# Stick-breaking attention: one PSUM bank of transposes for 256 queries of two heads instead of 512 queries of one

## The chip, the cores and the metric

One core of one Trainium2 chip. The metric is device time in microseconds (us) of one execution of the whole program; of the kernel before there are three such times, and one further execution was run under the profiler.

## What is computed

One encoder layer over 2048 tokens of width 1024. Stage 1 projects the input and runs eight RWKV-7 heads, stage 2 is stick-breaking attention over eight heads of 64, stage 3 is the output projection and a squared-ReLU MLP. The change is in stage 2, whose reference is (float32 throughout):

```python
for blk in range(T // Q_BLOCK):
    z = jnp.einsum('bhqd,bhkd->bhqk', q[:, :, start:end], k[:, :, :end]) * scale
    causal = jnp.arange(end)[None, :] < (start + jnp.arange(Q_BLOCK))[:, None]
    log_beta = jax.nn.log_sigmoid(z)
    log_keep = jnp.where(causal, log_beta - z, 0.0)
    log_a = log_beta + lax.cumsum(log_keep, axis=3, reverse=True) - log_keep
    att = jnp.where(causal, jnp.exp(log_a), 0.0)
    outs.append(jnp.einsum('bhqk,bhkd->bhqd', att, v[:, :, :end]))
```

The last line is the value product: for every query a weighted sum of the values of all earlier keys.

## The kernel before

Stage 2 (`stage2`, from L244) works on two heads at a time (a head pair `hp`, four of them), on 512 queries at a time (`b`, four blocks), and for each of these on 512 keys at a time (`j` from `b` down to 0). That makes 4 x (1+2+3+4) = 40 blocks: 16 diagonal ones (`j==b`), where only keys up to the query count, and 24 full ones.

`front` (L265) takes 128 queries (`i`, four per block). TensorE (PE) multiplies them with up to 512 keys for both heads (L271, tile `z`, two PSUM banks; the two heads take rows 0 to 63 and rows 64 to 127 of the array). On a diagonal block a mask is added (L273). ScalarE (ACT) makes two sigmoids of it (L275 `keep`, L277 `ga`), VectorE (DVE) the running product along the keys (L281 `E`, one scan per head), GpSimd (POOL) the product `ga*E` in place (L282). `ga` then holds the attention weights, queries in the partitions. It has 9 buffers of both heads, `z` has 2, `E` 6.

`back` (L285) takes 128 of the block's keys (`kt`, four per block). For each head PE transposes the 128x128 pieces of `ga` of all four `i` into one PSUM bank (L294, tile `tr`, 128 keys x 512 queries, two banks in turn), and the bank is copied to SBUF (tile `th`, 4 buffers): every fourth copy by DVE (L297), the others by ACT (L298). When both heads are through, PE multiplies the values with `th` and adds into `OT` (L301; head 0 into partitions 0 to 63, head 1 into partitions 64 to 127 of one bank). On a diagonal block `kt` needs only the queries from `128*kt` on, so the widths are 512, 384, 256 and 128. `finish` (L302) moves `OT` out after the last block of a head pair.

`step` (L313) issues the `front` of a new block and the `back` of the block before it in turn, `i` by `i`. That is the order in which the program is written. A scheduler then puts the instructions of each engine into a fixed order by a planned timeline; each engine runs its own queue in that order, and waits on semaphores for the others. In the trace a float32 matmul is two records (two passes), with a weight load each; a transpose is one record.

Of the kernel before, what the change touches and what calls it, by code (L numbers as in the profile page):

```python
# [8 lines left out]
F32 = mybir.dt.float32  # L9
# [234 lines left out]
def stage2(tc,consts,kd,qd,vd,sbd,cfg=None):  # L244

    nc=tc.nc; V_=nc.vector; A=nc.scalar; P=nc.gpsimd; TE=nc.tensor
    g=dict(GA=9,E=6,TH=4,QB=3,DV=4)
    g.update(cfg or {})
    with ExitStack() as ctx:
        sp=ctx.enter_context(tc.tile_pool(name="s2",bufs=1,reuse_waits="tile"))  # L250
        pz=ctx.enter_context(tc.tile_pool(name="p2z",bufs=1,reuse_waits="tile",space=PS))
        pp=ctx.enter_context(tc.tile_pool(name="p2",bufs=1,reuse_waits="tile",space=PS))
        pt=ctx.enter_context(tc.tile_pool(name="p2t",bufs=1,reuse_waits="tile",space=PS,side="right"))

        keeps=[sp.tile([128,2,513],F32,name=f"keep{i}") for i in range(2)]
        for k in keeps: P.memset(k[:,:,512:513],1.0)

        pad=pp.tile([128,1],F32,name="pad"); V_.memset(pad,0.0)
        kv={}; cnt=[0,0]
        def load(hp,j):  # L260
            K=sp.tile([128,512],F32,name=f"K{hp}{j}"); V=sp.tile([128,4,128],F32,name=f"V{hp}{j}")
            nc.sync.dma_start(out=K,in_=kd[hp][:,512*j:512*j+512])
            nc.sync.dma_start(out=V,in_=vd[hp][:,4*j:4*j+4])
            kv[hp,j]=(K,V)
        def front(b,hp,j,Q,carry,i):  # L265

            n=f"{b}{hp}{j}"; K=kv[hp,j][0]
            W=128*(i+1) if j==b else 512; o=512-W
            z=pz.tile([128,2,512],F32,tag="z",name=f"z{n}{i}",bufs=2)
            for h in range(2):  # L270
                TE.matmul(z[:,h,0:W],lhsT=Q[64*h:64*h+64,128*i:128*i+128],rhs=K[64*h:64*h+64,0:W],start=True,stop=j<b,skip_group_check=True)  # L271
            if j==b:
                for h in range(2): TE.matmul(z[:,h,W-128:W],lhsT=consts['identr'],rhs=consts['cmask'],start=False,stop=True,skip_group_check=True)  # L273
            s=keeps[cnt[0]%2]; cnt[0]+=1
            A.activation(s[:,:,o:512],z[:,:,0:W],AF.Sigmoid,scale=-0.125)  # L275
            ga=sp.tile([128,2,512],F32,tag="ga",name=f"ga{n}{i}",bufs=g['GA'])
            A.activation(ga[:,:,o:512],z[:,:,0:W],AF.Sigmoid,scale=0.125)  # L277
            E=sp.tile([128,2,513],F32,tag="E",name=f"E{n}{i}",bufs=g['E'])
            for h in range(2):
                init=1.0 if j==b else carry[i][h]  # L280
                V_.tensor_tensor_scan(E[:,h,o:513][:,::-1],s[:,h,o:513][:,::-1],pad.to_broadcast([128,W+1]),init,ALU.mult,ALU.bypass)  # L281
            P.tensor_tensor(out=ga[:,:,o:512],in0=ga[:,:,o:512],in1=E[:,:,o+1:513],op=ALU.mult)  # L282
            carry[i]=[E[:,h,o:o+1] for h in range(2)]
            return ga,o
        def back(b,hp,j,gas,OT,kt):  # L285

            n=f"{b}{hp}{j}"; V=kv[hp,j][1]
            i0=kt if j==b else 0; q0=128*i0
            ths=[]
            for h in range(2):  # L290
                tr=pt.tile([128,512],F32,tag="tr",name=f"tr{n}{kt}{h}",bufs=2)
                for i in range(i0,4):
                    ga,o=gas[i]
                    TE.transpose(tr[:,128*i:128*i+128],ga[:,h,o+128*kt:o+128*kt+128],consts['ident'])  # L294
                th=sp.tile([128,512],F32,tag="th",name=f"th{n}{kt}{h}",bufs=g['TH'])
                cnt[1]+=1
                if cnt[1]%g['DV']==0: V_.tensor_copy(out=th[:,q0:],in_=tr[:,q0:])  # L297
                else: A.copy(th[:,q0:],tr[:,q0:])  # L298
                ths.append(th)
            for h in range(2):  # L300
                TE.matmul(OT[64*h:64*h+64,q0:],lhsT=V[:,kt,64*h:64*h+64],rhs=ths[h][:,q0:],start=j==b and kt==0,stop=j==0 and kt==3,skip_group_check=True)  # L301
        def finish(b,hp,OT):  # L302
            n=f"{b}{hp}"
            ots=sp.tile([128,512],F32,tag="ots",name="ots"+n,bufs=2)
            V_.tensor_copy(out=ots,in_=OT)
            o=pt.tile([128,4,128],F32,tag="tr",name="o"+n,bufs=2)
            for i in range(4): TE.transpose(o[:,i],ots[:,128*i:128*i+128],consts['ident'])
            osb=sp.tile([128,4,128],F32,tag="osb",name="osb"+n,bufs=2)
            A.copy(osb,o)  # L309
            nc.sync.dma_start(out=sbd[512*b:512*b+512,128*hp:128*hp+128].rearrange("(i p) d -> p i d",i=4),in_=osb)  # L310

        late=[None]
        def step(new):  # L313
            prev,late[0]=late[0],new
            for i in range(4):
                if new:
                    b,hp,j,Q,carry,gas,st=new
                    gas.append(front(b,hp,j,Q,carry,i))
                if prev:
                    b,hp,j,Q,carry,gas,st=prev  # L320
                    if j==b and i==0: st.append(pp.tile([128,512],F32,tag="OT",name=f"OT{b}{hp}",bufs=1))
                    back(b,hp,j,gas,st[0],i)
                    if j==0 and i==3: finish(b,hp,st[0])
        for b in range(4):
            for hp in range(4):
                load(hp,b)
                Q=sp.tile([128,512],F32,tag="Q",name=f"Q{b}{hp}",bufs=g['QB'])
                nc.sync.dma_start(out=Q,in_=qd[hp][:,512*b:512*b+512])
                carry=[None]*4; st=[]
                for j in range(b,-1,-1): step((b,hp,j,Q,carry,[],st))  # L330
        step(None)
# [334 lines left out]
def hybrid_block(tc, x, smalls, w_in, wd, wa, wg, g1, g2, gnw, gnb, w_out, w_up, w_down, gf, out):  # L666
    nc = tc.nc
    with ExitStack() as ctx:
        cp = ctx.enter_context(tc.tile_pool(name="c", bufs=1))
        dp = ctx.enter_context(tc.tile_pool(name="dr", bufs=1, space=bass.MemoryType.DRAM))  # L670
        c = mk_consts(tc, cp)
        dram = lambda name, shape: dp.tile(shape, F32, name=name)
        kd, qd = dram("kd", [4, 128, T]), dram("qd", [4, 128, T])
        vd = [dram(f"vd{h}", [128, 16, 128]) for h in range(4)]
        scr = {k: [[dram(f"scr{k}{b}{h}", [4, 4, 128, 32]) for h in range(2)] for b in range(4)] for k in "AX"}
        yd, vrd, gd, sbd = (dram(n, [T, 512]) for n in ("yd", "vrd", "gd", "sbd"))
        bond = dram("bond", [T, 8])
        x2d = dram("x2d", [T // 2, D])
        sb_consts(tc, cp, c)
        c["gain"] = cp.tile([128, 4], F32, name="gain")  # L680
        nc.sync.dma_start(out=c["gain"], in_=smalls[:, 34:38])
        with tc.tile_pool(name="c1", bufs=1, reuse_waits="tile") as c1:
            rw_consts(tc, c1, c, smalls, wd, wa)
            stage1(tc, c, x, w_in, kd, qd, vd, scr, yd, vrd, bond, gd, wg, g1)
        stage2(tc, c, kd, qd, vd, sbd)
        stage3(tc, c, x, (yd, vrd, bond, gd, sbd), w_out, g2, w_up, w_down, gf, gnw, gnb, c["gain"], out, x2d)
# [40 lines left out]
```

## Time and profile before

| | |
|---|---|
| three runs | 3447.58 us median, 3442.96 to 3448.63 |
| the profiled execution | 3452.84 us; its span, first to last instruction, 3450.8 us |
| stage 2 in that span | about 1120 to 1785 us |
| granted TensorE clock, mean of the span | 0.969 (1.0 is 2.4 GHz) |

A timeline line has the start in us, the time in us that the merged records take together, engine, line, operation, output<-input and the count of records; in brackets the idle time of the engine before it and what ended it. Records of successive matmuls overlap at their ends, so the price of a group on PE is read from its start to the start of the next group, not from its own length. "PEld" is the weight load. A groups line has the count, the busy time in us, the mean of one record in ns, and the idle time before it by what ended it.

### The profile page before, as it was taken

Reading aid. Unit: us, or ns where it says so; the run is one execution under the profiler, and the core shown is the slowest. Engines: PE = TensorE matmul, PEld = TensorE weight load, DVE = VectorE, ACT = ScalarE, POOL = GpSimd, SP = SyncE. Lnnn points to the kernel's source line nnn. Section 1 sums busy time; section 2 is a strip of 40 time slices with the busy share of each in tenths; the row PEclk is TensorE's granted clock in tenths of the full one; section 3 lists DMA queues with packets and bytes.
Section 4 is the critical chain, followed back from the end, with each engine's and each line's share of the span. In section 5 each row is a group of like instructions: output and inputs, shape, how many; then the busy total and the mean of one; then the engine's idle time right before and its main releaser. Section 6 shows DMA issues by size and latency. Waiting matters only on the chain. (4 is left out here: it accounts for less than half of the span.)

```text
span 3450.8 us, 44556 instructions
## 1 busy us (share of the span) xinstructions
PE 3288.2 (95%) x16992; PEld 2403.2 (70%) x16992; DVE 1999.8 (58%) x3111; ACT 1194.3 (35%) x2252; POOL 1245.6 (36%) x1089
## 2 busy tenths in 40 slices
PE   8999989999997899999968999999999999999998
PEld 6677768777776433333326878888888878888887
DVE  4773574575473555565647655555555655555556
ACT  4434444444441566666642221111111321111112
POOL 5444444444440434444436632222222332222223
PEclk9999999999996899999988999999999999999999
DMA  3342342342231400000025421111111231111111
GB/s 99 100 126 66 95 120 72 88 124 73 83 99 31 134 16 13 13 10 7 4 73 183 141 92 49 49 49 49 49 49 49 93 121 46 47 48 49 49 49 61
DMA packets 146726, 239.24 MB, mean 69 GB/s; under 512 B 50000, under 2 KB 58192, under 8 KB 146512
## 3 DMA queue, kind: packets, MB, share of 16 engines
q1 hardware_dynamic: 146512, 236.39, 21.8%
q8 instruction: 134, 2.20, 0.3%
q14 instruction: 80, 0.66, 0.1%
HBM read 190.14 MB, written 46.20 MB: 68 GB/s over the span
## 5 line engine op out<-in xcount | busy, mean ns | idle before, releaser
L160 DVE TENSOR_TENSOR acc<-acc,dn 128x512 f32<-128x512 f32 x512 | 344.7, 685 | 413.7 <-PE dn L32 407.3
L282 POOL TENSOR_TENSOR ga<-ga,E 128x1024 f32<-128x1024 f32 (+3 forms) x160 | 274.7, 1726 | 381.5 <-ACT ga L277 272.2
L301 PE MATMUL OT<-th,V 128*64 128x512 f32 (+3 forms) x640 | 299.5, 554 | 3.0 <-DVE th L297 3.0
L145 ACT ACTIVATE r<-up 128x512 f32<-128x512 f32 x128 | 75.6, 592 | 615.4 <-PE up L32 615.4
L281 DVE TENSOR_TENSOR_SCAN E<-keep,E,pad 128x513 f32<-128x513 f32 x192 | 232.1, 1264 | 62.6 <-ACT keep L275 62.6
L294 PEld LDWEIGHTS tr<-ident,ga 128*128 128x128 f32 x1088 | 115.5, 141 | 206.4 <-issue 197.9
L148 DVE TENSOR_TENSOR m<-r 128x512 f32<-128x512 f32 x128 | 190.9, 1492 | 113.6 <-ACT r L145 113.6
L294 PE MATMUL tr<-ident,ga 128*128 128x128 f32 x1088 | 189.3, 289 | 1.0 <-ACT osb L309 1.0
L271 PE MATMUL z<-K,Q 64*128 64x512 f32 (+3 forms) x640 | 161.3, 589 | 25.3 <-ACT ga L277 17.0
L275 ACT ACTIVATE keep<-z 128x1024 f32<-128x1024 f32 (+3 forms) x160 | 144.7, 905 | 97.4 <-PE z L273 32.6
L298 ACT COPY th<-tr 128x512 f32<-128x512 f32 (+2 forms) x240 | 127.1, 535 | 129.2 <-PE tr L294 128.6
L149 DVE TENSOR_TENSOR gl<-m,gh 128x512 fp32r<-128x512 f32 x128 | 148.4, 1160 | 11.6 <-ACT gh L146 0.9
L277 ACT ACTIVATE ga<-z 128x1024 f32<-128x1024 f32 (+3 forms) x160 | 141.0, 895 | 31.5 <-PE tr L294 27.3
L281 DVE TENSOR_TENSOR_SCAN E<-keep,pad 128x129 f32<-128x129 f32 (+3 forms) x128 | 97.4, 806 | 66.9 <-ACT keep L275 55.6
L297 DVE COPY th<-tr 128x512 f32<-128x512 f32 (+1 forms) x80 | 46.2, 577 | 137.6 <-PE tr L294 137.2
L301 PEld LDWEIGHTS OT<-th,V 128*64 128x64 f32 x640 | 61.1, 134 | 92.7 <-issue 41.9
L532 DVE TENSOR_TENSOR tm<-Am,Xs 128x240 f32<-128x240 f32 (+27 forms) x248 | 110.9, 447 | 23.4 <-DMA Am<-scrA 17.2
L383 POOL TENSOR_TENSOR wls<-wfs,whs 128x512 fp32r<-128x512 f32 x64 | 84.6, 1322 | 104.0 <-ACT whs L382 96.8
L533 DVE TENSOR_TENSOR Xs<-Xs,tm 128x240 f32<-128x240 f32 (+27 forms) x248 | 114.3, 461 | 6.3
L30 PE MATMUL ips<-hT,whs 128*128 128x512 f32 x256 | 106.8, 417 | 0.5 <-ACT whs L382 0.5
L32 PE MATMUL ips<-hT,wls 128*128 128x512 f32 x256 | 105.9, 414 | 0.9 <-POOL wls L383 0.9
L30 PE MATMUL op<-wo,yh 128*128 128x512 f32 x256 | 103.1, 403 | 3.0 <-ACT yh L116 3.0
(1265 smaller groups left out, 8677.4 us busy)
## 6 DMA issues: line engine op xcount, KB each, us to landing
wfs<-w_in SPq DMA_DIRECT2D x64, 256.0 KB, 2.9
x<-x SPq DMA_DIRECT2D x32, 256.0 KB, 3.0
wfr<-w_in SPq DMA_DIRECT2D x32, 256.0 KB, 2.8
wfk<-w_in SPq DMA_DIRECT2D x32, 256.0 KB, 2.7
wfv<-w_in SPq DMA_DIRECT2D x32, 256.0 KB, 2.8
wfsv<-w_in SPq DMA_DIRECT2D x32, 256.0 KB, 2.9
x<-x SPq DMA_DIRECT2D x16, 512.0 KB, 3.4
out<-fo SPq DMA_DIRECT2D x32, 256.0 KB, 2.5
```

What stands on the lines that cost most here:

```text
L30: nc.tensor.matmul(ps,lhsT=lh,rhs=rh,start=first,stop=False)
L148: V.tensor_tensor(out=m,in0=r,in1=r,op=ALU.mult)
L149: V.tensor_tensor(out=gl[:,bl],in0=m,in1=gh[:,bl].bitcast(F32),op=ALU.subtract)
L160: V.tensor_tensor(out=a,in0=a,in1=ps,op=ALU.add)
L271: TE.matmul(z[:,h,0:W],lhsT=Q[64*h:64*h+64,128*i:128*i+128],rhs=K[64*h:64*h+64,0:W],start=True,stop=j<b,skip_group_check=True)
L275: A.activation(s[:,:,o:512],z[:,:,0:W],AF.Sigmoid,scale=-0.125)
L277: A.activation(ga[:,:,o:512],z[:,:,0:W],AF.Sigmoid,scale=0.125)
L281: V_.tensor_tensor_scan(E[:,h,o:513][:,::-1],s[:,h,o:513][:,::-1],pad.to_broadcast([128,W+1]),init,ALU.mult,ALU.bypass)
L282: P.tensor_tensor(out=ga[:,:,o:512],in0=ga[:,:,o:512],in1=E[:,:,o+1:513],op=ALU.mult)
L294: TE.transpose(tr[:,128*i:128*i+128],ga[:,h,o+128*kt:o+128*kt+128],consts['ident'])
L298: else: A.copy(th[:,q0:],tr[:,q0:])
L301: TE.matmul(OT[64*h:64*h+64,q0:],lhsT=V[:,kt,64*h:64*h+64],rhs=ths[h][:,q0:],start=j==b and kt==0,stop=j==0 and kt==3,skip_group_check=True)
```

## The change

Instead of one bank per head with all queries, `back` now makes one bank per half of the queries (`u`, 256 queries) with both heads side by side. A half that lies wholly ahead of `kt` on a diagonal block is left out. The bank is copied in one step, and both heads' value products, now 256 queries wide, follow that copy. The copies go to DVE at three places in eight instead of two in eight.

```diff
-    g=dict(GA=9,E=6,TH=4,QB=3,DV=4)
+    g=dict(GA=9,E=6,TH=4,QB=3,DV=(1,4,7))
...
-            ths=[]
-            for h in range(2):
-                tr=pt.tile([128,512],F32,tag="tr",name=f"tr{n}{kt}{h}",bufs=2)
-                for i in range(i0,4):
-                    ga,o=gas[i]
-                    TE.transpose(tr[:,128*i:128*i+128],ga[:,h,o+128*kt:o+128*kt+128],consts['ident'])
-                th=sp.tile([128,512],F32,tag="th",name=f"th{n}{kt}{h}",bufs=g['TH'])
+            for u in range(2):
+
+                c0=max(i0,2*u)
+                if c0>=2*u+2: continue
+                tr=pt.tile([128,2,256],F32,tag="tr",name=f"tr{n}{kt}{u}",bufs=2)
+                for h in range(2):
+                    for i in range(c0,2*u+2):
+                        ga,o=gas[i]
+                        TE.transpose(tr[:,h,128*(i-2*u):128*(i-2*u)+128],ga[:,h,o+128*kt:o+128*kt+128],consts['ident'])
+                th=sp.tile([128,2,256],F32,tag="th",name=f"th{n}{kt}{u}",bufs=g['TH'])
+                q=slice(128*(c0-2*u),256); qq=slice(128*c0,256*u+256)
                 cnt[1]+=1
-                if cnt[1]%g['DV']==0: V_.tensor_copy(out=th[:,q0:],in_=tr[:,q0:])
-                else: A.copy(th[:,q0:],tr[:,q0:])
-                ths.append(th)
-            for h in range(2):
-                TE.matmul(OT[64*h:64*h+64,q0:],lhsT=V[:,kt,64*h:64*h+64],rhs=ths[h][:,q0:],start=j==b and kt==0,stop=j==0 and kt==3,skip_group_check=True)
+                if cnt[1]%8 in g['DV']: V_.tensor_copy(out=th[:,:,q],in_=tr[:,:,q])
+                else: A.copy(th[:,:,q],tr[:,:,q])
+                for h in range(2):
+                    TE.matmul(OT[64*h:64*h+64,qq],lhsT=V[:,kt,64*h:64*h+64],rhs=th[:,h,q],start=j==b and kt==0 and u==0,stop=j==0 and kt==3 and u==1,skip_group_check=True)
```

The prediction also speaks of two other groups of matmuls, in stage 1: L574 writes its eight heads in turn into partitions 0 to 63 and 64 to 127, L579 writes its eight heads all into the same 64 partitions.

```python
574:                    TE.matmul(Sp[64*j:64*j+64,h//2],lhsT=BT[cc][:,e,j],rhs=UV[cc][:,e,h],start=h<2,stop=True,skip_group_check=True)
579:                    TE.matmul(X[vb:vb+64,h],lhsT=P1[cc][:,e,h%2,cr:cr+64],rhs=UV[cc][:,e,h],start=False,stop=h==7,skip_group_check=True)
```

## Rows read from the trace of the kernel before

**Rows 1.** Busy time of each engine by stretch: stage 2.

```profile
core 0: us, PE busy (x) PEld busy (x) DVE busy (x) ACT busy (x) POOL busy (x), PEclk, DMA share, GB/s
1120.00:1785.00 665.00, 632.42 (x2570) 254.60 (x2568) 381.15 (x417) 398.79 (x578) 274.66 (x160) 0.98 0.08 26
```

**Rows 2.** Groups by line and shape, stage 2.

```profile
L301 PE MATMUL OT<-th,V 128*64 128x512 f32 x448 | 237.5, 618 | 0.0
L281 DVE TENSOR_TENSOR_SCAN E<-keep,E,pad 128x513 f32<-128x513 f32 x192 | 232.1, 1264 | 62.6 <-ACT keep L275 62.6
L298 ACT COPY th<-tr 128x512 f32<-128x512 f32 x176 | 104.0, 591 | 119.6 <-PE tr L294 119.4
L297 DVE COPY th<-tr 128x512 f32<-128x512 f32 x48 | 32.9, 685 | 113.1 <-PE tr L294 113.1
L301 PEld LDWEIGHTS OT<-th,V 128*64 128x64 f32 x640 | 61.1, 134 | 92.7 <-issue 41.9 <-ACT th L298 31.6 <-DVE th L297 13.8
```

**Rows 3.** Timeline of a full block's back, head pair 0 of b=2.

```profile
1316.20 1.07 PE L301 MATMUL OT<-th,V 128*64 128x512 f32 x2
1316.36 0.58 ACT L298 COPY th<-tr 128x512 f32<-128x512 f32 x1 [0.56 <-PE tr L294]
1317.20 0.66 PE L294 MATMUL tr<-ident,ga 128*128 128x128 f32 x4
1317.79 1.07 PE L301 MATMUL OT<-th,V 128*64 128x512 f32 x2
```

**Rows 4.** Timeline of PE on a diagonal block: the narrower groups.

```profile
1305.21 0.86 PE L301 MATMUL OT<-th,V 128*64 128x384 f32 x2
1306.00 0.44 PE L294 MATMUL tr<-ident,ga 128*128 128x128 f32 x2
...
1308.59 0.65 PE L301 MATMUL OT<-th,V 128*64 128x256 f32 x2
1309.16 0.33 PE L294 MATMUL tr<-ident,ga 128*128 128x128 f32 x1
1309.42 1.13 PE L271 MATMUL z<-K,Q 64*128 64x512 f32 x4
...
1311.32 0.43 PE L301 MATMUL OT<-th,V 128*64 128x128 f32 x2
1311.68 0.66 PE L294 MATMUL tr<-ident,ga 128*128 128x128 f32 x4
```

**Rows 5.** Timeline of PE in stage 1: L574 and L579.

```profile
252.30 0.69 PE L574 MATMUL Sp<-UV,BT 128*64 128x64 f32 x16
252.82 1.10 PE L579 MATMUL Xp<-UV,P 128*64 128x64 f32 x16
253.85 0.33 PE L612 MATMUL tri<-ident,x 128*128 128x128 f32 x1
```

**Rows 6.** Timeline, end of a head pair: both heads' products side by side.

```profile
1324.15 1.93 PE L301 MATMUL OT<-th,V 128*64 128x512 f32 x4
1324.25 0.69 DVE L297 COPY th<-tr 128x512 f32<-128x512 f32 x1 [5.31 <-PE tr L294]
1325.00 0.19 PEld L301 LDWEIGHTS OT<-th,V 128*64 128x64 f32 x2 [0.66 <-DVE th L297]
```

**Rows 7.** Timeline of PE: `z` of two heads over 256 keys, and what follows.

```profile
1341.69 0.70 PE L271 MATMUL z<-K,Q 64*128 64x256 f32 x4
1342.33 0.44 PE L273 MATMUL z<-cmask,identr 128*128 128x128 f32 x2
```

**Rows 8.** Timeline where a new query block begins (b=2).

```profile
1328.31 9.50 DVE L281 TENSOR_TENSOR_SCAN E<-keep,E,pad 128x513 f32<-128x513 f32 x8 [1.50 <-ACT keep L275]
1331.00 1.13 PE L271 MATMUL z<-K,Q 64*128 64x512 f32 x4 [0.70 <-ACT ga L277]
...
1335.22 1.13 PE L271 MATMUL z<-K,Q 64*128 64x512 f32 x4 [1.02 <-ACT ga L277]
```

**Rows 9.** Groups, whole span: the weight loads of L574.

```profile
L574 PEld LDWEIGHTS Sp<-UV,BT 128*64 128x64 f32 x512 | 20.9, 158 | 14.2 <-issue 7.1 <-ACT UV L570 6.0 <-ACT pmr L429 0.4
```

## The prediction

> **What bounds the kernel now.** I read the busy time by stretch first, because only stage 2 changes. Over its 665 us PE is busy 632 us, ACT 399, DVE 381, POOL 275, and the granted clock is 0.98 [rows 1]. So PE is the engine to watch. The groups by line then say what fills it: the value products of L301 [rows 2]. The timeline shows how PE goes through a full block: a product of one head, four transposes, a product, with no gap [rows 3]. The price of a group is the distance to the start of the next one: 1.00 us for a 512-wide product, 0.59 for four transposes [rows 3]; 0.79, 0.57 and 0.36 us for products 384, 256 and 128 wide, and 0.26 for one transpose [rows 4]. By differences a product costs about 0.15 us plus 0.0017 per column, a transpose group 0.15 plus 0.11 each, so two cost 0.37 and three 0.48.
>
> Today the two heads' products stand apart: each waits for its own copy, and transposes fill the time between. The change puts them next to each other. All turns on whether two products that use different halves of the array's columns run at the same time.
>
> **The change part by part.** *Do neighbours overlap?* No line of stage 2 shows it. Where both heads do stand together the four records take 1.93 us, nearly twice one product's 1.07, but the second head's weight load starts only when its DVE copy is through (1324.25 + 0.69 = 1324.94, load at 1325.00) [rows 6], so that proves nothing. Stage 1 has the same form, 128 rows by 64 columns, both ways: L574, alternating between the column halves, gets 16 records off in 0.52 us; L579, always in one half, needs 1.03 us [rows 5]. Two halves run side by side at half the price. So a pair of 256-wide products should cost hardly more than one alone, 0.57 us. The dearer bound is `z`, two heads side by side in the rows, 0.64 us at 256 columns [rows 7]; the dearest is one after the other, 0.57 + 256 x 0.0017 = 1.00 us. I take 0.57, as L574 has the very form and `z` has another.
>
> *Products.* Removed: 320, of which 224 are 512 wide (24 full blocks x 8, 16 diagonal ones x 2) and 32 of each narrower width: 224 x 1.00 + 32 x (0.79 + 0.57 + 0.36) = 279 us. Added: 288 pairs, 256 of them 256 wide (24 x 8 + 16 x 4) and 32 with 128: 256 x 0.57 + 32 x 0.36 = 157 us. Difference -122 us, all on PE. With the price of `z` (0.64, and 0.07 more for the narrow ones too) it is -101; with no overlap 256 x 1.00 + 32 x 0.57 = 274, or -5.
>
> *Transposes.* Their number stays 1088, in fewer groups: before 224 x 0.59 + 32 x (0.48 + 0.37 + 0.26) = 168, after 256 x 0.59 + 32 x 0.37 = 163 us: -5.
>
> *Weight loads.* 640 become 1152. One takes 134 ns [rows 2], a pass over 256 columns 213 (half of 0.0017 x 256), so a load is hidden under the pass before it: nothing, unless loads can't run under a neighbour's pass (a rival below).
>
> *Copies.* 320 become 288, each of at most 512 elements as now, 0.59 us on ACT and 0.685 on DVE [rows 2]. DVE gets 108 in place of 80, at most 28 x 0.685 = 19 us more (381 to 400); ACT 180 in place of 240, at most 35 us less. Both stay under PE's 632 - 127 = 505 us. What they cost is waiting. The copy starts 0.16 us after the product that follows its transposes [rows 3], and PE wants it after that product and four transposes: 1.59 us now, 0.57 + 0.59 = 1.16 then. The slack of a DVE copy falls from about 0.70 to 1.16 - 0.16 - 0.685 - 0.05 = 0.27 us (0.05 from a copy's end to PE's start, [rows 6]). It stands in DVE's queue behind scans of 1.264 us [rows 2], which fill over half of DVE's time then (about 330 of 580 us, estimated as 381 less 80 copies). A copy that meets a scan at random meets one 0.57 of the time, and is late by (1.264 - 0.27)^2 / (2 x 1.264) = 0.39 us on average: 108 x 0.57 x 0.39 = 24 us, against about 5 by the same sum today. +19. Behind a late copy stand all later PE work and, through `z`, the sigmoids; a planned order could make it 0, a bad one twice as much.
>
> *Where PE already waits.* At the start of a query block eight scans run in one piece for 9.5 us, and PE waits for `ga` to free a `z` bank, 0.70 and 1.02 us [rows 8]. There ACT and DVE set the pace, so products made shorter only lengthen those waits. About four pairs fall into such a stretch, each 1.00 - 0.57 = 0.43 us, at 16 query blocks: +27. It is 0 if other transposes fill in, and 40 x 4 x 0.43 = 69 if it holds for every one of the 40 blocks.
>
> No DMA, POOL or SP instruction is touched; SP's queue and POOL's product keep their places. Stages 1 and 3 stay.
>
> *Sum.* -122 - 5 + 19 + 27 = **-81 us**. Against the profiled execution's 3452.8 that is 3372; the runs' median lies 5.3 below it, so the forecast is 3447.6 - 81 = **3367 us**.
>
> **A rule that speaks against it.** Each load of L574 takes 158 ns, 512 of them 81 us, but they occupy only 20.9 us: about four are under way at once [rows 9], and its pairs share all 128 rows. The Trainium skill, "TensorE: Matmul & The Clock Gate", Part 3 (What overlaps and what doesn't), says that weight loads go under running matmuls only when the row group differs; the two heads here use the same rows. By that rule the sum would be the last rival's; the trace disagrees with it as far as 64-wide matmuls go.
>
> **The rivals.** *The front takes it back.* PE gets shorter, but the wait seen at query-block starts appears in all 40 blocks: -122 - 5 + 19 + 69 = -39, 3408 us. For it: DVE would be at 400 and ACT at up to 399 of some 600 us, with only two `z` banks. Against: in the full blocks today both stand idle during long runs of products (the ACT copy and DVE copies there wait for PE 119 and 113 us) [rows 2].
>
> *The heads don't run together,* because something is scheduled between them or because it holds for short matmuls alone: -5 - 5 = -10, 3438 us. Against: both wait for the same copy and follow each other in the program, and [rows 5].
>
> *Loads are exposed: slower.* If the second head's first load can't start before the first head's passes end, each of 288 pairs pays 134 ns in place of an overlap: 39 - 10 = +29, 3477 us. The place is the array between the heads. It decides against the change as soon as 10 / 0.134 = 75 of the 288 pairs pay it without overlapping. Against it stands [rows 9]; the products of one head too have 640 x 134 ns = 86 us of loads in 61 us [rows 2].
>
> **How the numbers follow.** A measurement of this kernel tells about 0.2%, 7 us, from no change. Forecast 0.70; front 0.14; not together 0.09, half of it within 0.2% since it is only 10 us; loads exposed 0.07. So faster 0.88, within 0.2% 0.05, slower 0.07. The range: at the fast end the two give-backs of 46 us shrink to a third (-111, 3337); at the slow end it takes in the `z` price with all give-backs (-101 - 5 + 46 = -60, 3388), the front rival at 3408, and some us of it being worse, 3415. What is left out is the two last rivals and an end of the front one, about 0.2.
>
> **What would show it.** Right: L301 comes in fours, 256 wide, with 0.57 to 0.64 us to the next group, where nothing is waited for; stage 2 ends some 80 us earlier, near 1705; PE's idle time there grows by about 46 us, on copies by DVE and on `ga`. Wrong: fours at 1.00 us (not together), more than 1.00 (loads), or short fours with idle time of over 80 us between (front). A granted clock below 1.0 in stage 2 would be something I have not counted.

## The result, and the profile after

The changed kernel takes 3342.8 us (median of four runs, 3338.5 to 3349.0) against 3447.9 of the kernel before beside it: 0.970 of it, 95% interval 0.968 to 0.972, or 105 us less. The forecast was 3367 (range 3337 to 3415): the direction and the main mechanism, two heads' products at the same time, came out; the gain is 24 us larger than the sum of 81, because one term of the give-back was wrong (see below).

Line numbers from L294 on are three or four higher in the changed kernel: transposes L297, DVE copies L301, ACT copies L302, products L304, `ots` L308, `o` L310. The busy time by stretch, each cut, to within 0.6 us, from its first `z` to its last transpose of an output; the upper line is the kernel before, the lower the changed one (columns as in [rows 1]):

```profile
1129.30:1783.00 653.70, 630.81 (x2557) 253.42 (x2558) 380.84 (x416) 396.34 (x575) 274.66 (x160) 0.99 0.07 24
```

```profile
1122.90:1666.60 543.70, 507.24 (x3072) 247.74 (x3072) 397.95 (x444) 369.19 (x515) 274.53 (x160) 0.99 0.09 29
```

Stage 2 is 110 us shorter. PE's busy time falls by 124 us (forecast 127), its idle time grows from 22.9 to 36.5 us, by 14 (forecast 46). POOL does the same work; DVE has 17 us more, ACT 27 less. The rest of the span, 2797.1 and 2793.0 us, differs by 4 us between these two executions. Some 4 of the 124 us are not the change's: the first 8.6 us of stage 2 ran at a granted clock of 0.50 (1.2 GHz) in this execution, the first 16.7 us in the one before, and the rest at 1.00. In a second profile of the changed kernel (e8 below) the clock rose only at 1147 us, as late as before; there PE's busy time is 118 us below the kernel before and stage 2 is 105 us shorter.

A full block's back in the changed kernel, timeline, to be laid beside [rows 3]:

```profile
1307.44 0.20 PEld L304 LDWEIGHTS OT<-th,V 128*64 128x64 f32 x4 [0.17 <-issue]
1307.44 0.65 PE L304 MATMUL OT<-th,V 128*64 128x256 f32 x4
1307.55 0.59 ACT L302 COPY th<-tr 128x512 f32<-128x512 f32 x1 [0.85 <-PE tr L297]
1308.03 0.66 PE L297 MATMUL tr<-ident,ga 128*128 128x128 f32 x4
1308.61 0.65 PE L304 MATMUL OT<-th,V 128*64 128x256 f32 x4
1308.72 0.69 DVE L301 COPY th<-tr 128x512 f32<-128x512 f32 x1 [1.64 <-PE tr L297]
1309.20 0.66 PE L297 MATMUL tr<-ident,ga 128*128 128x128 f32 x4
```

Four records, two heads of 256 queries, are 0.59 us from the next group (1307.44 to 1308.03), hardly more than the 0.57 us of one 256-wide product before [rows 4]. The period of a product and a transpose group is 1.17 us in place of 1.59. All four weight loads are off within 0.20 us at the start of the group.

The groups of stage 2 that answer to [rows 2]:

```profile
L304 PE MATMUL OT<-th,V 128*64 128x256 f32 x1024 | 166.1, 404 | 17.0 <-DVE th L301 16.6 <-ACT th L302 0.2
L302 ACT COPY th<-tr 128x512 f32<-128x512 f32 x160 | 93.9, 590 | 73.2 <-PE tr L297 72.2
L301 DVE COPY th<-tr 128x512 f32<-128x512 f32 x96 | 65.0, 677 | 58.7 <-PE tr L297 53.5 <-ACT th L302 4.2
L304 PEld LDWEIGHTS OT<-th,V 128*64 128x64 f32 x1152 | 57.6, 134 | 103.4 <-issue 40.1 <-DVE th L301 31.4 <-ACT th L302 14.6
L271 PE MATMUL z<-K,Q 64*128 64x512 f32 x448 | 125.0, 641 | 3.0 <-ACT ga L277 2.7
```

Each copy takes what it took. The products now wait 17 us for DVE copies, and `z` waits hardly at all for `ga`. From the waits of stage 2, the kernel before first, the changed one second (us in total, times, longest):

```profile
PE z L271 <- ACT ga L277: 17.0, 27, 1.0
PE OT L301 <- DVE th L297: 3.0, 9, 0.9
PE o L307 <- DVE ots L305: 1.6, 2, 0.8
```

```profile
PE OT L304 <- DVE th L301: 17.8, 32, 1.4
PE o L310 <- DVE ots L308: 9.0, 10, 1.1
PE z L271 <- ACT ga L277: 3.3, 6, 0.7
```

So the waits have moved: from the `z` banks to copies that stand in DVE's queue. In all 32 waits for `th` the copy follows directly on a scan; one of them:

```profile
1421.86 1.26 DVE L281 TENSOR_TENSOR_SCAN E<-keep,E,pad 128x513 f32<-128x513 f32 x1
1423.03 0.66 DVE L301 COPY th<-tr 128x512 f32<-128x512 f32 x1
1423.75 0.65 PE L304 MATMUL OT<-th,V 128*64 128x256 f32 x4 [1.36 <-DVE th L301]
```

By place the picture is another. From 6 us before to 10 us after the 16 groups of output transposes (`o`), where one query block gives way to the next, PE's idle times add up to 20.7 us before and 23.5 in the changed kernel, though the instruction that waits is another. Here the changed kernel passes the point that [rows 8] shows of the kernel before:

```profile
1327.16 0.65 PE L304 MATMUL OT<-th,V 128*64 128x256 f32 x4
1327.74 1.13 PE L271 MATMUL z<-K,Q 64*128 64x512 f32 x4
1328.80 0.65 PE L304 MATMUL OT<-th,V 128*64 128x256 f32 x4
1329.39 1.13 PE L271 MATMUL z<-K,Q 64*128 64x512 f32 x4
1331.50 0.66 PE L310 MATMUL o<-ident,ots 128*128 128x128 f32 x4 [0.98 <-DVE ots L308]
```

Products stand between the `z` groups, none of them waits, and PE waits for `ots` instead. Everywhere else in stage 2 PE's idle time rises from 2.1 to 12.8 us, 11.7 of them waits for DVE's copies.

### The profile page after: what moved, and what is told of

It reads as the page before. It is cut to its first block, busy times and chain, and to the rows that moved or that the text cites. A ratio compares the mean times of both kernels' runs of the same rounds, so it can differ in the third digit from the quotient of the medians.

```text
span 3336.7 us, 45433 instructions
## 1 busy us (share of the span) xinstructions
PE 3166.1 (95%) x17504; PEld 2398.0 (72%) x17504; DVE 2010.7 (60%) x3139; ACT 1167.7 (35%) x2192; POOL 1245.4 (37%) x1089
## 5 line engine op out<-in xcount | busy, mean ns | idle before, releaser
L304 PE MATMUL OT<-th,V 128*64 128x256 f32 (+1 forms) x1152 | 179.5, 392 | 18.2 <-DVE th L301 17.8
L297 PEld LDWEIGHTS tr<-ident,ga 128*128 128x128 f32 x1088 | 114.5, 140 | 105.6 <-issue 94.1
L297 PE MATMUL tr<-ident,ga 128*128 128x128 f32 x1088 | 181.5, 287 | 5.4 <-DVE th L301 2.2
L304 PEld LDWEIGHTS OT<-th,V 128*64 128x64 f32 x1152 | 57.6, 134 | 103.4 <-issue 40.1
L302 ACT COPY th<-tr 128x512 f32<-128x512 f32 (+1 forms) x180 | 101.2, 566 | 75.8 <-PE tr L297 74.7
L301 DVE COPY th<-tr 128x512 f32<-128x512 f32 (+1 forms) x108 | 69.8, 647 | 63.1 <-PE tr L297 57.9
```

Source lines behind the costliest of these rows:

```text
L297: TE.transpose(tr[:,h,128*(i-2*u):128*(i-2*u)+128],ga[:,h,o+128*kt:o+128*kt+128],consts['ident'])
L304: TE.matmul(OT[64*h:64*h+64,qq],lhsT=V[:,kt,64*h:64*h+64],rhs=th[:,h,q],start=j==b and kt==0 and u==0,stop=j==0 and kt==3 and u==1,skip_gr ...
```

## The experiments

Eleven runs followed, two of them repeats (e8, e11). Times are medians, ratios are to the kernel before on the same chip.

| run | edit | us | ratio, 95% interval | PE busy / idle in stage 2, us |
|---|---|---|---|---|
| before | | 3447.9 | 1 | 630.8 / 22.9 |
| changed kernel | | 3342.8 | 0.970 (0.968 to 0.972) | 507.2 / 36.5 |
| e1_same_columns | both heads in one column half | 3426.4 | 0.994 (0.992 to 0.996) | 608.7 / 25.0 |
| e2_dve_quarter | 2 copies of 8 on DVE | 3334.5 | 0.968 (0.966 to 0.969) | 513.5 / 32.3 |
| e3_before_dve38 | before, 3 copies of 8 on DVE | 3452.7 | 1.002 (1.001 to 1.003) | 632.7 / 23.6 |
| e4_two_copies | one copy per head | 3350.8 | 0.973 (0.970 to 0.975) | 531.7 / 28.5 |
| e5_no_dve | all copies on ACT | 3328.0 | 0.965 (0.963 to 0.966) | 513.6 / 23.7 |
| e6_third_bank | zero column in SBUF, 3 banks | 3455.1 | 1.002 (1.001 to 1.004) | 555.3 / 106.6 |
| e7_pad_in_sbuf | zero column in SBUF, 2 banks | 3508.0 | 1.017 (1.015 to 1.019) | 581.5 / 128.3 |
| e8_after_again | changed kernel, control | 3344.4 | 0.970 (0.968 to 0.973) | 512.3 / 36.7 |
| e9_no_dve_ots_act | e5, and `ots` on ACT | 3339.9 | 0.968 (0.966 to 0.970) | 513.2 / 33.7 |
| e10_one_dve_ots_act | e9, 1 copy of 8 on DVE | 3338.5 | 0.968 (0.966 to 0.970) | 514.8 / 31.5 |
| e11_no_dve_again | e5, control | 3323.8 | 0.964 (0.962 to 0.965) | 508.2 / 23.5 |

The same program's PE busy time differs by some 5 us from one profiled execution to another (507.2 and 512.3, 513.6 and 508.2): the granted clock of stage 2 is 0.99 in the shorter and 0.98 in the longer of each pair. Differences of that size between runs are not read below.

### Is the gain the overlap?

```diff
+                    hh=h if j==b and kt==0 else 0
-                    TE.matmul(OT[64*h:64*h+64,qq],...)
+                    TE.matmul(OT[64*hh:64*hh+64,qq],...)
```

> The changed kernel, but the second head's product goes to the same partitions (and so the same half of the array's columns) as the first head's, except at the first key tile of a head pair; the second head's result is therefore left out of its place. Bank layout, copies and number of instructions stay. Theory (the gain is the two products running at the same time in different column halves): the fours of records, 256 wide, go from 0.58 to 1.00 us to the next group; 272 of 288 pairs x 0.42 = 114 us more work on PE, less some 10 to 20 us of waits for copies that get their slack back: 3343 + 100 = about 3440 us. Rival (the gain comes from fewer waits or from the balance of the copies): within 10 us of 3343.

Measured 3426.4 us, 83 above the changed kernel. The timeline of PE in this run (the products stand at L305 here):

```profile
1306.28 1.08 PE L305 MATMUL OT<-th,V 128*64 128x256 f32 x4
1307.29 0.65 PE L297 MATMUL tr<-ident,ga 128*128 128x128 f32 x4
1307.87 1.08 PE L305 MATMUL OT<-th,V 128*64 128x256 f32 x4
1308.88 0.66 PE L297 MATMUL tr<-ident,ga 128*128 128x128 f32 x4
```

The same four records, with the same two weight matrices and the same `th`, now take 1.01 us, the price of one after the other, once both go to the same column half. (A column half and the 64 partitions that it writes go together, and the run can't tell them apart. That both products add into the same places of `OT` is not needed for it: L579 writes different places of one half, and its products do not overlap either [rows 5].) The expectation counted 272 such pairs; the edit leaves the 32 pairs of each diagonal block's first key tile as they were, so it is 224 wide pairs x 0.42 + 32 narrow ones x 0.21 = 101 us. PE's busy time is 101 us above the changed kernel's. As the groups got longer, the copies got slack back and idle time fell by 11.5 us. The overlap is thus worth 83 us of the 105 by itself, net of the copies' slack; this kernel's remaining 20 us against before hold the fewer groups (10 by the prediction's sum) and the 32 pairs that still overlap (32 x 0.42 = 13).

### Does the one-step copy bring the heads together?

```diff
+                for h in range(2):
-                if cnt[1]%8 in g['DV']: V_.tensor_copy(out=th[:,:,q],in_=tr[:,:,q])
-                else: A.copy(th[:,:,q],tr[:,:,q])
+                    if cnt[1]%8 in g['DV']: V_.tensor_copy(out=th[:,h,q],in_=tr[:,h,q])
+                    else: A.copy(th[:,h,q],tr[:,h,q])
```

> The changed kernel, but each head's half of the bank is copied by an instruction of its own (same engine for both). The scheduler then has the two products ready at different times; in the queue of PE some 40 of 288 pairs come apart. Theory (together means overlap): each pair that is apart pays 0.42 us, 18 us; the copies add about 0.16 us to 288 steps, and PE waits longer for them: 3343 + 18 + 20 to 50 = about 3395. Rival (the one-step copy itself is what gains, the overlap little): most of the 105 us is lost, above 3420.

Measured 3350.8 in two runs, so 6 to 8 us above the changed kernel, not 50, and the intervals of the two overlap. In the trace 34 products stand alone and 10 groups hold three; from group to group the products of stage 2 take 179.5 us in place of 160.8, so 19 more, as the 18 of the expectation say. The second half of the expectation fell: PE's waits did not grow with the longer copying, idle time was 28.5 us instead of 36.5. One copy for both heads helps to keep them together, but most pairs stay together without it. In the kernel before, with a bank and a copy for each head, 200 of the 224 products 512 wide stand alone. So it is probably the common bank that brings the two heads together, as it makes both products ready at nearly the same time.

### What did PE's waits hang on?

```diff
-    g=dict(GA=9,E=6,TH=4,QB=3,DV=(1,4,7))
+    g=dict(GA=9,E=6,TH=4,QB=3,DV=(0,4))
```

> The changed kernel with two copies in eight on VectorE, as before the change, instead of three. Theory (PE's waits for a z bank went from 17 to 3 us because ScalarE has 60 copies fewer): with 216 copies on ScalarE those waits come back to 10 us or more while the waits for VectorE copies fall from 20 to about 13; the time stays within 7 us of 3343. Rival (the z waits went because the order of the queues changed with the shorter products): z waits stay under 6 us, VectorE waits fall by a third, and the time is 5 to 10 us shorter, about 3335.

Measured 3334.5. The waits for `z` banks stayed away with 216 copies on ACT (0.2 us for the 512-wide ones), so ACT's load is not what removed them. The waits for DVE copies did not fall by a third either: with 72 such copies in place of 108 the products still wait 18.0 us, so the total does not go by the number of copies. The intervals of this run (0.966 to 0.969) and of the changed kernel (0.968 to 0.972) touch, on different chips; its 8 us are not settled.

```diff
-    g=dict(GA=9,E=6,TH=4,QB=3,DV=4)
+    g=dict(GA=9,E=6,TH=4,QB=3,DV=(1,4,7))
...
-                if cnt[1]%g['DV']==0: V_.tensor_copy(out=th[:,q0:],in_=tr[:,q0:])
+                if cnt[1]%8 in g['DV']: V_.tensor_copy(out=th[:,q0:],in_=tr[:,q0:])
```

> The kernel before with three copies in eight on VectorE, nothing else. Theory (share of the copies): PE's waits for a z bank fall from 17 us to 6 or less, the time by about 10 us to 3438. Rival (order of the queues, or the shorter products): waits and time as before, 3448 within 5 us, or a little longer by VectorE copies behind scans.

Measured 3452.7, 1.002 of the kernel before (1.001 to 1.003): nothing gained. Its waits:

```profile
PE o L307 <- DVE ots L305: 13.3, 13, 1.4
PE OT L301 <- DVE th L297: 5.2, 18, 0.5
PE z L271 <- ACT ga L277: 3.2, 10, 0.8
```

The waits for `z` banks did fall, from 17.0 to 3.2 us, as the first theory had it, and the time did not follow: PE was idle for 23.6 us instead of 22.9, now behind `ots` and copies. Near the output transposes the idle times add up to 21.6 us, against 20.7. Those 17 us moved to other instructions, by a new order of the queues or because DVE got the work that ACT lost (the run does not tell), and the sum stayed. The new share of the copies alone is worth nothing.

### Can the waits that the change made be taken away?

```diff
-    g=dict(GA=9,E=6,TH=4,QB=3,DV=(1,4,7))
+    g=dict(GA=9,E=6,TH=4,QB=3,DV=())
```

> The changed kernel with all 288 copies on ScalarE. Theory (the 36 us that PE stands idle in stage 2 come mostly from copies that stand behind 1.26 us scans on VectorE): those 20 us of waits go, ScalarE (about 440 of 525 us) is still under PE's 507, the time falls by 10 to 20 us against the changed kernel run beside it. Rival (any engine that copies is busy with long work; a copy behind a 1.03 us sigmoid is late as well): waits for VectorE turn into waits for ScalarE and for z banks, time within 7 us or longer.

Measured 3328.0, 16 us below the changed kernel run beside it (3344.4):

```profile
1126.00:1663.30 537.30, 513.59 (x3072) 248.99 (x3072) 335.25 (x336) 418.16 (x623) 274.79 (x160) 0.98 0.09 29
```

```profile
L304 PE MATMUL OT<-th,V 128*64 128x256 f32 x1024 | 167.9, 407 | 0.9 <-ACT th L302 0.7
L271 PE MATMUL z<-K,Q 64*128 64x512 f32 x448 | 127.9, 648 | 2.9 <-ACT ga L277 2.9
```

The products' waits fall from 17 us to 0.9, and only part of that comes back elsewhere: the waits for `ots`, for `ga` and for ACT's copies grow by some 8 us together, against 20 us that go. ACT carries all 288 copies within 418 of 537 us. PE's idle time is back to 23.7 us, as in the kernel before; near the output transposes it is 21.8, elsewhere 1.8. The theory holds: what the change gave back was copies behind scans on DVE. The control beside it, on that chip:

> The changed kernel itself, as a control on the same chip as the three others: 3343 us within 7 us, and about 8 us above the run with two copies in eight on VectorE (3334) if that difference is the kernel's and not the chip's.

It came out at 3344.4, as expected for the kernel itself, and 10 us above e2, which ran on another chip.

```diff
-        pad=pp.tile([128,1],F32,name="pad"); V_.memset(pad,0.0)
+        pad=sp.tile([128,1],F32,name="pad"); V_.memset(pad,0.0)
...
-                tr=pt.tile([128,2,256],F32,tag="tr",name=f"tr{n}{kt}{u}",bufs=2)
+                tr=pt.tile([128,2,256],F32,tag="tr",name=f"tr{n}{kt}{u}",bufs=3)
...
-            o=pt.tile([128,4,128],F32,tag="tr",name="o"+n,bufs=2)
+            o=pt.tile([128,4,128],F32,tag="tr",name="o"+n,bufs=3)
```

> The changed kernel with three banks for the transposes instead of two; the zero column that the scans read moves from PSUM to SBUF to make room. Theory (what is left idle on PE is slack: 0.27 us for a VectorE copy with two banks, about 1.4 us with three): PE's waits for copies fall from 20 us to under 5, the time by 10 to 20 us against the changed kernel beside it. Rival (with products this short ScalarE and VectorE set the pace in stretches, banks don't matter): under 7 us.

The first line of that diff alone:

> Only the zero column of the scans moves from PSUM to SBUF; two banks as in the changed kernel. Both theories: scans stay at 1.26 us each and the time within 5 us of the changed kernel beside it; if a scan gets longer by 0.1 us, 320 scans are 32 us of VectorE's time, of which a part shows, and the run with three banks is to be read against this one.

Measured 3455.1 and 3508.0, both far off. With the zero column in SBUF the scans are longer on the mean; from the groups of the second of these runs, and its stretch:

```profile
L281 DVE TENSOR_TENSOR_SCAN E<-keep,E,pad 128x513 f32<-128x513 f32 x192 | 341.7, 1829 | 38.4 <-ACT keep L275 38.4
L282 POOL TENSOR_TENSOR ga<-ga,E 128x1024 f32<-128x1024 f32 x112 | 245.0, 2193 | 292.4 <-DVE E L281 152.1 <-ACT ga L277 74.1 <-PE tr L297 33.8
L304 PE MATMUL OT<-th,V 128*64 128x256 f32 x1024 | 189.0, 453 | 94.7 <-DVE th L301 92.4 <-ACT th L302 2.1
```

```profile
1129.30:1839.00 709.70, 581.45 (x3072) 278.45 (x3072) 546.75 (x444) 371.67 (x515) 302.59 (x160) 0.87 0.07 22
```

A scan takes 1.829 us on the mean in place of 1.264 and DVE is busy for 547 us, so PE waits for its copies for 92 us, and the granted clock over stage 2 falls to 0.87. But a scan by itself is no dearer. The shortest, the median and the longest of the 192 scans, in ns, and one long scan with the POOL product beside it:

```profile
L281 DVE TENSOR_TENSOR_SCAN E<-keep,E,pad x192: 1250/1262/3030, 1192.9 to 1821.3; 128x513 f32<-128x513 f32 x192
```

```profile
1388.65 2.10 POOL L282 TENSOR_TENSOR ga<-ga,E 128x1024 f32<-128x1024 f32 x1 [3.13 <-ACT ga L277]
1388.88 2.95 DVE L281 TENSOR_TENSOR_SCAN E<-keep,E,pad 128x513 f32<-128x513 f32 x1
```

The 83 scans that met no POOL product took 1.258 us on the mean, as before; the 109 that met one took 2.264. What costs time, with the column in SBUF, is a scan and a POOL product at once. Against this control the third bank gains 53 us (3455.1 of 3508.0), with 22 us less idle time, the products' waits for DVE's copies down from 98 to 80 us, and a clock of 0.90. So slack for the copies is worth something when they are late, but no run has a third bank with the column left in PSUM, and what three banks would give the changed kernel stays open.

### A faster version, and where it ends

> The version with all 288 copies on ScalarE and ots on VectorE once more, as the control of the two others: 3328 us within 7 us, 0.965 of the kernel before.

> All 288 copies and also the 16 copies of the finished output (ots) on ScalarE. Theory (on VectorE a copy that PE waits for stands behind scans): PE's 11 us of waits for ots shrink to under 5, ScalarE gets 11 us more; the time is 5 to 10 us below the kernel with all copies on ScalarE and ots on VectorE, run beside it. Rival (ScalarE, at 418 of 537 us, is by now the one that is late): no gain, or waits for ScalarE grow by as much.

```diff
-            V_.tensor_copy(out=ots,in_=OT)
+            A.copy(ots,OT)
```

> One copy in eight on VectorE, the rest and ots on ScalarE. Theory: 36 copies behind scans cost about a third of the 18 us that 108 cost, 6 us, so it is 3 to 8 us above the version with none. Rival (ScalarE late): it is the fastest of the three, by 3 us or more.

The version with all copies on ACT came out again at 3323.8 us, 0.964 (0.962 to 0.965). Moving `ots` too made it 16 us slower (3339.9): PE's 11 us of waits for `ots` went, but others came; from the waits of that run:

```profile
PE tr L297 <- ACT osb L312: 16.1, 12, 1.7
PE z L271 <- ACT ga L277: 13.0, 29, 0.9
```

The waits are for ACT now, as the rival said. One copy of eight back on DVE did not mend it: 3338.5 is no different from 3339.9, and neither side of that run's expectation came out. So ACT's load is not what makes it late. With 409 us of work, less than the 418 of the version with `ots` on DVE, PE still waits 12.7 us for `osb` and 10.9 for `ga`, against 1.1 and 4.8 there. The trace of e9 points at the order of ACT's queue:

```profile
1295.21 0.66 PE L310 MATMUL o<-ident,ots 128*128 128x128 f32 x4
1296.37 1.03 ACT L275 ACTIVATE keep<-z 128x1024 f32<-128x1024 f32 x1 [0.86 <-PE tr L297]
1297.30 0.58 ACT L312 COPY osb<-o 128x512 f32<-128x512 f32 x1
1298.02 0.63 PE L297 MATMUL tr<-ident,ga 128*128 128x128 f32 x4 [1.71 <-ACT osb L312]
```

The copy `osb` could start when the transposes of `o` are through, at 1295.87; ACT stands idle, but a sigmoid that waits comes first in its queue, and PE's next transposes need the bank that `osb` frees. No run changes that order alone. The best version of the study is the changed kernel with all value copies on ACT and `ots` on DVE: 15 to 19 us below the change, and its interval lies wholly below the change's.

## Why the prediction was right or wrong

*Neighbours overlap.* Right, and at the price taken: 0.57 was put in, 0.59 is read. The argument from L574 and L579 [rows 5] held for products four times as wide, and e1 shows that the column half (with its partitions) is the cause and not the order or the bank.

*Products and transposes,* -122 and -5. Right: from group to group the products take 160.8 us in place of 279.6 and the transposes 166.3 in place of 169.9, -119 and -4. PE's busy time fell by 124 us (118 in e8, where the granted clock rose as late as before).

*Weight loads,* nothing. Right: 1152 x 134 ns = 154 us of loads occupy 57.6 us, and a group costs hardly more than one head's; in e1, with both heads in one half, as many loads occupy 124.1 us. The rule of the Trainium skill, "TensorE: Matmul & The Clock Gate", Part 3 (What overlaps and what doesn't), under which the second head's loads would have been exposed, does not hold for two column halves with the same rows: all four loads of a pair are off within 0.20 us, while the first passes run.

*Copies,* +19. Right in cause: PE's waits for DVE copies rose from 3.0 to 17.8 us, each behind a scan, and e5 takes them away. That the size is near, 15 of 19, is in part luck: the sum has 108 x 0.57 = 62 late copies of 0.39 us, measured are 32 waits of 0.56 on the mean, and with two thirds of the copies (e2) they add up to the same. Not named was `ots`, the other DVE copy that PE waits for: 1.6 to 9.0 us.

*Where PE already waits,* +27. This is the term that failed. It took the waits for a `z` bank [rows 8] for a pace set by ACT and DVE, which shorter products can only lengthen. They fell from 17.0 us to about 3, and the idle time at these places, whatever PE waits for there, grew by 3 us (20.7 to 23.5), or by 1 with all copies on ACT (e5: 21.8). e3 shows the same in the old layout: a different share of the copies takes the `z` waits away, `ots` takes their place, and the sum stays. So the idle time at the ends of query blocks did not grow with the shorter products; the order of the queues decides at which instruction it shows, and in e9, with `ots` on ACT, also how much it is (32.0 us). Why it did not grow, no run shows. With the term at zero and the others as they stood the sum would have been -108; the stage became 110 us shorter in the first profile and 105 in e8's, with PE's idle time up by 14 in place of 46.

The rivals: "the front takes it back" (3408) fell with that term. "Not together" is what e1 builds; apart from the 32 pairs it leaves overlapping (13 us), its 20 us agree with the 10 forecast. "Loads are exposed" fell.

## What to carry to other kernels

Two matmuls that each use half of the array's columns are worth putting next to each other in PE's queue: arrange their data so that both become ready by the same step, and look for a pair elsewhere in the same trace, in the same column half and in different ones, to price it beforehand. When PE's groups get shorter, redo the slack of every copy that stands behind long work on another engine; here ACT took all of them, and that gave another 0.5%. The load of an engine does not tell whether it is late: a copy can stand behind a waiting instruction on an engine that is idle. A wait seen on the busiest engine is not yet a pace that grows when its work shrinks: add up its idle time at that place, whatever instruction it stands at, and compare that sum between variants.

## What the runs showed of the hardware that was not expected

The scans read a zero operand, one column broadcast. With that column in PSUM it made no difference whether a POOL product ran at the same time: 1.264 us per scan of 513 elements with one and 1.260 without, in the changed kernel. With the column in SBUF (e7) a scan that met no product took 1.258 us and one that met a product 2.264, and a POOL product of 1024 elements that met a scan 2.228 in place of 1.997 us. In the lines shown the scan starts 0.23 us into the product and ends 1.08 us after it.

With PE idle for up to 4.9 us at a time in that run the granted clock of stage 2, a mean over stretches at 1.2 and at 2.4 GHz, was 0.87, against 0.98 to 0.99 in the runs with the column in PSUM, whose idle times there are 1.7 us at most.
